# A decoder layer on one core: other column chunks in three stages, and another order of the three passes in two MLP groups

## The chip, the core and the metric

The kernel runs on one core of a Trainium2 chip. The core has a matrix engine (TensorE; PE in the profile, its weight loads PEld), a vector engine (DVE), a scalar engine (ACT), a general-purpose engine (POOL) and queues that issue transfers (SP's above all). The engines run side by side and wait for each other by semaphores. The metric is the device time of one execution in microseconds. Before the change three runs gave 2565.99, 2566.34 and 2569.97 us, a median of 2566.34.

## The reference

One layer of a decoder is applied to 1024 prompt tokens and to 64 sampled tokens (8 sequences of 8): 1088 columns in all, with 1024 channels. Four token mixers run in parallel on one input projection. The change touches only what follows them: the four branch projections with their gates, the output projection, and the MLP.

```python
branches = jnp.stack([y_hg, y_rw, y_cf, y_lru], axis=2).astype(dt)
bo = jnp.einsum("btkc,kcd->btkd", branches, p["w_branch"][l])
gates = jax.nn.sigmoid((h @ p["w_gate"][l] + p["b_gate"][l]).reshape(bsz, t, N_BRANCH, D_MODEL))
out = jnp.sum(gates * bo, axis=2) @ p["w_out"][l]
...
x = x + g1 * out
h2 = rmsnorm(x, p["norm_mlp_g"][l]) * (1.0 + sc2) + sh2
x = x + g2 * (jnp.square(jax.nn.relu(h2 @ p["w_mlp1"][l])) @ p["w_mlp2"][l])
```

Everything is float32, and the MLP's hidden layer has 4096 channels.

## The kernel before

Channels lie on the 128 partitions and tokens on the columns, so a tensor of 1024 channels is eight tiles (k-tiles) of 128 x 1088. A weight matrix is cut into 128 x 128 blocks. One output tile (an m-tile) is the sum over its k-tiles.

**Three passes.** Large products are computed from rounded operands. `split` (L206) writes `hi`, a rounded copy in the type float32r, with ACT, and `lo` = source - `hi` with DVE. `weights` (L148) fetches four k-tiles of weights at a time into `wst` and splits them into `whi` and `wlo`; there are three buffers for the first and four for each of the others. `products` (L158) then issues three matmuls for each k-tile into one sum: whi x hi, wlo x hi, whi x lo.

**Column chunks.** A PSUM bank holds 512 float32 columns, so 1088 columns are done in chunks. `CHUNKS` (L25) has 364, 362 and 362 columns. `gemm` (L169) goes over groups of four k-tiles, in each over the chunks, in each over four k-tiles of three passes, 12 matmuls for a chunk. The sums lie in the pool `pg`, which has three banks. After a chunk's last k-tile its evacuation reads the bank, with a high priority.

**Stages after the mixers.**

- Branch projections (L1131): four branches of eight m-tiles, four k-tiles each. DVE multiplies the sum by the gate `gt` and adds it to `M`.
- Output projection (L1168): eight m-tiles, eight k-tiles each. Before it, `M` is split into `Mh` and `Ml`, by `CHUNKS`: the first chunk of all eight k-tiles, then the second, then the third (L1160). The evacuation is `add_resid` (L1140), which adds the gated sum to the residual `R`, the 1024 prompt columns in one instruction and the 64 sampled columns in two, and `add_sq` (L1149), which squares `R` on ACT (into `sqt`) and adds it to `accs` on DVE.
- Second norm: `rms_finish` (L288) sums `accs` over the partitions on TensorE, by `CHUNKS`. ACT makes `rstd` of it, and DVE, POOL and ACT make `u`, then the MLP's input `Gh` and `Gl`.
- MLP: eight groups of 512 hidden channels. In each, four m-tiles of first products (L1223, eight k-tiles), whose evacuation is a ReLU and a square on ACT and two DVE instructions that leave `ah` and `al`; then eight m-tiles of second products (L1227, four k-tiles), evacuated by `add_resid`. Group 0 does its first two m-tiles chunk by chunk, and group 7's second products run by columns with the final norm behind them.

Code is written in program order; a scheduler of the framework sets each engine's order from priorities and its own estimates of time. Each engine then works strictly in that order.

Of the kernel before, what the change touches and what calls it, by code (L numbers as in the profile page):

```python
# [24 lines left out]
CHUNKS = ((0, 364), (364, 362), (726, 362))  # L25
DECAY = 0.606531
# [4 lines left out]
# packed per-channel parameters: name -> (first column, columns)  # L31
# [11 lines left out]
# constants that depend on shapes alone: name -> (first column, columns)  # L43
# [43 lines left out]
class Net:  # L87
    def __init__(self, ctx, tc, A):
        self.ctx, self.tc, self.nc, self.A = ctx, tc, tc.nc, A
        self.slots = list(range(13))  # L90

# [21 lines left out]
    def flat(self, name, slot):  # L113
        """one of this round's slots, each with a tile at a time"""
        return self.fp.tile([128, 1120], F32, name=name, tag=f"f{self.slots[slot]}", bufs=1)
# [32 lines left out]
    def weights(self, ap, prio=True):  # L148
        """four k-tiles of weights, rounded and remaining parts"""
        with self.tc.high_priority(offset=PRIO) if prio else nullcontext():  # L150
            st = self.wp.tile([128, 4, 128], F32, name="wst", tag="wst", bufs=WST)
            hi = self.wp.tile([128, 4, 128], F32R, name="whi", tag="whi", bufs=WHI)
            lo = self.wp.tile([128, 4, 128], F32R, name="wlo", tag="wlo", bufs=WHI)
            self.nc.sync.dma_start(st, ap)
            self.split(hi, lo, st)
        return hi, lo

    def products(self, ps, n0, n, W, X, k0, kt, nk=4):  # L158
        """nk k-tiles' three passes"""
        hi, lo = W  # L160
        xh, xl = X
        for k in range(k0, k0 + nk):
            i = k % 4
            a, b = xh(k)[:, n0:n0 + n], xl(k)[:, n0:n0 + n]
            self.mm(ps[:, :n], hi[:, i, :], a, start=k == 0, stop=False)
            self.mm(ps[:, :n], lo[:, i, :], a, start=False, stop=False)
            self.mm(ps[:, :n], hi[:, i, :], b, start=False, stop=k == kt - 1)
# [13 lines left out]
    def gemm_cols(self, items, X):  # L181
        """two m-tiles (weights, evacuation) of eight k-tiles, column chunk by column chunk"""
        Ws = [[self.weights(ap[:, k0:k0 + 4, :]) for k0 in (0, 4)] for ap, _ in items]
        for n0, n in CHUNKS:
            for W, (_, evac) in zip(Ws, items):
                ps = self.pgt("pg")
                for h in range(2):
                    self.products(ps, n0, n, W[h], X, 4 * h, 8)
                with self.tc.high_priority(offset=PRIO):
                    evac(ps, n0, n)  # L190

    def gemm_first(self, items, Ws, X):
        """two m-tiles of eight k-tiles, two k-tiles at a time, as they come"""
        pss = [[f("pg") for f in (self.pgt, self.pmt)] for _ in CHUNKS]
        for k in range(0, 8, 2):
            for (n0, n), pp in zip(CHUNKS, pss):
                for ps, W, (_, evac) in zip(pp, Ws, items):
                    self.products(ps, n0, n, W[k // 4], X, k, 8, 2)
                    if k == 6:
                        with self.tc.high_priority(offset=PRIO):  # L200
                            evac(ps, n0, n)
# [4 lines left out]
    def split(self, hi, lo, src):  # L206
        """src -> hi (rounded) and lo = src - hi, both float32r."""
        self.act(hi, src)
        self.tt(lo, src, hi.bitcast(F32), OP.subtract)

    def log_table(self, after=()):
        """from here on the activation table that has both Ln and Exp"""
        load = self.nc.scalar.preload_act_table_set("natural_log_exp_and_others")
        self.tc.keep_in_program_order(load)
        for i in after:
            self.after(load, i)
# [4 lines left out]
    def exph(self, out):  # L221
        """out holds ln(x); x^-1/2"""
        return self.act(out, out, AF.Exp, scale=-0.5)

    def after(self, i, j):
        """i is queued behind j"""
        self.tc.add_manual_dep(i.ins, j.ins.name, mybir.DependencyInfo(
            mybir.DependencyClass.NoSync, mybir.DependencyReason.DATA), reason="activation table")

# [8 lines left out]
    def ada_chunk(self, n, pool, pieces):  # L238
        """columns n*512..+512 of silu(c) @ ada_w + ada_b, channel-major into self.mod."""
        self.ada_sums(n, self.ada_parts(n, pool, pieces))  # L240
# [16 lines left out]
    def ada_sums(self, n, part, psum=None):  # L257
        """the first four chunks hold two k-tiles of shift, then the same two of scale"""
# [9 lines left out]
    def scale_from(self, g, sc, k0=0, n=8):  # L268
        """g * (1 + scale), in place in self.mod's columns sc*8+k0..+n"""
        m = self.mod[:, sc * 8 + k0:sc * 8 + k0 + n, :]  # L270
        g = PV[g] + k0
        self.stt(m, m, 1.0, self.pv[:, g:g + n].unsqueeze(2).to_broadcast([128, n, 9]), OP.add, OP.mult)
# [7 lines left out]
    def sumsq(self, acc, x, tmp):  # L280
        """acc += x^2 (acc = x^2 where tmp is None)"""
# [6 lines left out]
    def rms_finish(self, acc, out, chunks=CHUNKS):  # L288
        """out = rsqrt(sum over partitions of acc / D + eps), on every partition"""
# [6 lines left out]
    def split_mod(self, t, u, sc, sh, kb, hi, lo):  # L296
        """samples: u = t * scale + shift, split into hi + lo"""
# [6 lines left out]
    def rw_init(self):  # L304
# [9 lines left out]
        # scan resets: 0 where a chunk (or a sampled sequence) starts  # L314
# [6 lines left out]
        # (I - A)^-1 A of each head, the other head's rows 0  # L321
# [6 lines left out]
    def rw_shift(self, *jobs, Ws=None):  # L328
        """project m-tile mt, mix with the previous token: x + (prev - x) * mu"""
# [42 lines left out]
    def rw_block(self, j):  # L372
# [7 lines left out]
        # operands by chunk: (a~, r~) and (k~, b~), tokens innermost; eight chunks to a tile, then the samples  # L380
# [24 lines left out]
        # kk's norm  # L405
# [30 lines left out]
        # k' = k * (1 + (a - 1) ka)  # L436
# [6 lines left out]
        # scores within a chunk; rows k | b, columns a | r  # L443
# [25 lines left out]
        # bonus  # L469
# [6 lines left out]
        # (I - A)^-1 : 32 x 32 diagonal blocks, one per partition  # L476
# [19 lines left out]
        # X1: rows 64-95 the first block's inverse, rows 96-127 A12^T X1; the inverses (transposed) replace A in G  # L496
# [21 lines left out]
        # chunks  # L518
# [8 lines left out]
        for c in [16] + list(range(16)):  # L527
# [24 lines left out]
            # U = X (A_ak V + A S^T)  # L552
# [18 lines left out]
            # state  # L571
# [15 lines left out]
            # outputs  # L587
# [28 lines left out]
        # group norm over each head's values, bonus, gate  # L616
# [16 lines left out]
    def hg_init(self):  # L633
# [3 lines left out]
        # lower bound: cumsum(softmax over layers) - softmax[0]; one layer  # L637
# [10 lines left out]
    def hg_block(self, h):  # L648
# [20 lines left out]
        # scores, one level of halving at a time: X = [k exp(ref - b) | q exp(b - ref)]  # L669
# [67 lines left out]
        # decay to the chunk's start and end  # L737
# [146 lines left out]
    def lru_init(self):  # L884
# [8 lines left out]
        # softplus(-lambda) = max(-lambda, 0) + log1p(exp(-|lambda|)), with  # L893
        # log1p(e) = 2 atanh(z), z = e / (2 + e) <= 1/3, odd series to z^25
# [22 lines left out]
    def lru_block(self, j):  # L917
# [33 lines left out]
        # sqrt(-expm1(2 la)) with -expm1(2 la) = tanh(-la) (1 + exp(2 la)), la = -8 rg softplus(-lambda)  # L951
# [32 lines left out]
def trunk_kernel(ctx: ExitStack, tc: tile.TileContext, A):  # L984
# [14 lines left out]
    # ---- conditioning and the first norm  # L999
# [51 lines left out]
    # ---- input projection and the mixers  # L1051
    gsc = {}
    with ExitStack() as m:
# [32 lines left out]
        for j, order in enumerate(ROUNDS):  # L1086
            for st in order:
                steps[st](j)
            # a round's slots by its own numbers, in the order in which this one leaves them
# [8 lines left out]
    # ---- branch projections, gated and summed  # L1098
    mctx = ExitStack()
    merged = None  # L1100
    with ExitStack() as m:
# [5 lines left out]
        for bi, b in enumerate(ORDER):  # L1107
# [10 lines left out]
            for mt in range(8):  # L1118
# [11 lines left out]

                net.gemm(A["w_br"][b * 8 + mt], 4, Y, ev)  # L1131

    # ---- output projection, second norm
# [6 lines left out]
    def add_resid(ps, n0, n, mt, gi):  # L1140
        e = min(n, T - n0)
        r = R[mt]
        net.stt(r[:, n0:n0 + e], ps[:, :e], net.modp(gi, mt), r[:, n0:n0 + e], OP.mult, OP.add)
# [5 lines left out]
    def add_sq(n0, n, mt):  # L1149
        t = rp.tile([128, 364], F32, name="sqt", tag="sqt", bufs=2)[:, :n] if mt else None  # L1150
        net.sumsq(accs[:, n0:n0 + n], R[mt][:, n0:n0 + n], t)

    with ExitStack() as m:
# [9 lines left out]
        for mt in range(8):  # L1163
# [4 lines left out]
            net.gemm(A["w_out"][mt], KB8, (lambda k: Mh[k], lambda k: Ml[k]), ev)  # L1168
# [26 lines left out]
    # ---- MLP  # L1195
    with ExitStack() as m:
        ap_ = m.enter_context(tc.tile_pool(name="ap", bufs=1, reuse_waits="tile"))
        X2 = (lambda k: Gh[k], lambda k: Gl[k])
        for g in range(8):
# [21 lines left out]
            for i in range(i0, 4):  # L1221
                w, ev = first(i)
                net.gemm(w, KB8, X2, ev)  # L1223
            Y = (lambda k, ah=ah: ah[k], lambda k, al=al: al[k])
            if g < 7:
# [3 lines left out]
            # the last group by columns, so that the final norm runs behind the products  # L1229
# [110 lines left out]
```

## Time and profile before

| | |
|---|---|
| runs (median; all) | 2566.34; 2565.99, 2569.97, 2566.34 us |
| span of the profiled execution, first to last instruction | 2565.8 us |
| mean granted TensorE clock | 0.989 |
| branch projections | about 1451 to 1664 us |
| output projection, first to last matmul start | 1665.2 to 1763.0 us |
| MLP, from the first matmul start | 1766.9 us |

The page gives busy time of each engine, the chain of waits that ended last, and groups of instructions by line and tile. A name such as `pg<-Mh,whi` reads "writes a tile of pg, reads Mh and whi"; `128x364` is the shape that is written or read. All matmuls of the large products have line 103, that of a helper, so they are told apart by tiles. A matmul's length in the trace contains the time in which it overlaps the next one; the time from one start to the next is what a product costs.

### The profile page before, as it was taken

To read this page: it belongs to the slowest core of one execution; us is meant where nothing else is said; L and a number is where in the kernel's file an instruction comes from. 1 tells how busy PE (TensorE), PEld (TensorE's weight loads), DVE (VectorE), ACT (ScalarE), POOL (GpSimd) and SP (SyncE) were. 2 spreads that over 40 slices of the span, in tenths; PEclk is the share of its full clock that TensorE was granted. 3 is DMA by queue.
4 is the path that set the end of the run, shared out by engine and by line. 5 is a ranking of instruction groups with operands and counts; after the bars stand their busy time and mean duration, and the time that the engine had idled before them with its cause. 6 is when DMAs were issued, how large, how long until landed. Compare 5 with 4: busy or idle time off the path is not lost.

```text
span 2565.8 us, 43032 instructions
## 1 busy us (share of the span) xinstructions
PE 2488.8 (97%) x17874; PEld 2291.9 (89%) x17874; DVE 1339.9 (52%) x2506; ACT 916.2 (36%) x1644; POOL 248.8 (10%) x375
## 2 busy tenths in 40 slices
PE   6999999999999999999999999998999999999997
PEld 2897898897898978989887999998999999999997
DVE  6664626637265554457552756646534434434437
ACT  4522434323454224452244653334221221221225
POOL 3101110102100021000011000004000000000003
PEclk9999999999999999999999999999999999999998
DMA  6323131222222222212213454510111111111113
GB/s 238 121 78 78 53 104 65 64 85 72 90 69 66 70 86 93 65 61 79 85 53 109 167 193 158 185 42 26 50 46 46 42 46 46 46 42 46 46 42 110
DMA packets 112450, 209.23 MB, mean 82 GB/s; under 512 B 34408, under 2 KB 40504, under 8 KB 112256
## 3 DMA queue, kind: packets, MB, share of 16 engines
q1 hardware_dynamic: 98064, 166.93, 21.3%
q0 software_dynamic: 10880, 34.32, 3.5%
q10 hardware_dynamic: 3312, 5.25, 0.6%
q8 instruction: 140, 2.29, 0.4%
q14 instruction: 54, 0.44, 0.1%
HBM read 164.89 MB, written 41.55 MB: 80 GB/s over the span
## 4 chain that ended last, share of the span: by engine, by line
PE 83%; DVE 10%; DMA 3%; ACT 2%; issue 1%; POOL 0%; DVEq 0%; ACTq 0%; SPq 0%; POOLq 0%
PE pg L103 67%; PE sm L103 3%; DVE X L97 2%; PE ada L103 2%; PE pu L103 2%; DMA zx<-At 1%; PE pyr L103 1%; PE G L103 1%; DVE wlo L97 1%; PE tr L103 1%; PE po L103 1%; PE tr L537 1%; PE pst L103 1%; DVE Zu L97 1%; DVE tm L97 1%
## 5 line engine op out<-in xcount | busy, mean ns | idle before, releaser
L103 PE MATMUL pg<-Hh,whi 128*128 128x362 f32 (+1 forms) x1872 | 628.0, 336 | 4.6 <-ACT Hh L94 4.2
L103 PE MATMUL pg<-Hh,wlo 128*128 128x362 f32 (+1 forms) x1872 | 631.1, 337 | 0.0
L103 PE MATMUL pg<-Hl,whi 128*128 128x362 f32 (+1 forms) x1872 | 623.2, 336 | 0.7 <-DVE Hl L100 0.6
L94 ACT ACTIVATE whi<-wst 128x512 fp32r<-128x512 f32 x340 | 213.1, 628 | 730.9 <-PE pg L103 721.8
L97 DVE TENSOR_TENSOR wlo<-wst,whi 128x512 fp32r<-128x512 f32 x340 | 237.2, 699 | 428.7 <-ACT whi L94 427.3
L103 PEld LDWEIGHTS pg<-Hh,whi 128*128 128x128 f32 x1872 | 356.1, 190 | 15.2 <-ACT Hh L94 6.0
L103 PEld LDWEIGHTS pg<-Hh,wlo 128*128 128x128 f32 x1872 | 356.8, 191 | 13.8 <-issue 6.5
L103 PEld LDWEIGHTS pg<-Hl,whi 128*128 128x128 f32 x1872 | 355.2, 190 | 10.7 <-issue 2.5
L103 PE MATMUL pg<-Gh,whi 128*128 128x362 f32 (+1 forms) x768 | 253.4, 330 | 3.5 <-ACT Gh L94 2.6
L103 PE MATMUL pg<-Gl,whi 128*128 128x362 f32 (+1 forms) x768 | 252.4, 330 | 4.4 <-DVE Gl L97 4.0
L103 PE MATMUL pg<-Gh,wlo 128*128 128x362 f32 (+1 forms) x768 | 253.1, 330 | 0.1
L103 PE MATMUL pg<-ah,whi 128*128 128x362 f32 (+1 forms) x768 | 252.6, 329 | 0.5 <-DVE t L97 0.5
L103 PE MATMUL pg<-ah,wlo 128*128 128x362 f32 (+1 forms) x768 | 252.4, 329 | 0.0
L103 PE MATMUL pg<-al,whi 128*128 128x362 f32 (+1 forms) x768 | 250.1, 327 | 0.0
L100 DVE SCALAR_TENSOR_TENSOR R<-pg,mod,R 128x364 f32<-128x364 f32 (+2 forms) x216 | 123.6, 572 | 196.8 <-PE pg L103 196.8
L100 DVE SCALAR_TENSOR_TENSOR cacc<-u,pv,cacc 128x1024 f32<-128x1024 f32 x120 | 154.2, 1285 | 2.1
L103 PEld LDWEIGHTS pg<-Gl,whi 128*128 128x128 f32 x768 | 145.4, 190 | 7.6 <-DVE Gl L97 7.3
L103 PEld LDWEIGHTS pg<-Gh,whi 128*128 128x128 f32 x768 | 144.9, 189 | 4.9 <-ACT Gh L94 3.5
L103 PEld LDWEIGHTS pg<-Gh,wlo 128*128 128x128 f32 x768 | 144.9, 189 | 0.4 <-DVE wlo L97 0.4
L103 PEld LDWEIGHTS pg<-ah,whi 128*128 128x128 f32 x768 | 144.2, 188 | 1.1 <-ACT sqt L94 0.8
L103 PEld LDWEIGHTS pg<-al,whi 128*128 128x128 f32 x768 | 144.7, 189 | 0.1
L103 PEld LDWEIGHTS pg<-ah,wlo 128*128 128x128 f32 x768 | 144.3, 188 | 0.1
(383 smaller groups left out, 3698.7 us busy)
## 6 DMA issues: line engine op xcount, KB each, us to landing
wst<-w SPq DMA_DIRECT2D x136, 256.0 KB, 2.6
wst<-w_in SPq DMA_DIRECT2D x92, 256.0 KB, 2.9
gt<-g SPq DMA_DIRECT2D x32, 544.0 KB, 3.8
wst<-w_gate SPq DMA_DIRECT2D x64, 256.0 KB, 3.6
adaw<-ada SPq DMA_DIRECT2D x32, 512.0 KB, 4.4
g<-gst POOLq DMA_DIRECT2D x64, 181.0 KB, 2.2
yst<-y SPq DMA_DIRECT2D x16, 544.0 KB, 4.8
adaw<-ada SPq DMA_DIRECT2D x32, 256.0 KB, 5.4
```

The lines of the kernel that those rows point to most:

```text
L94: return self.nc.scalar.activation(out, in_, func, bias=bias, scale=scale)
L97: return self.nc.vector.tensor_tensor(out, a, b, op=op)
L100: return self.nc.vector.scalar_tensor_tensor(out, a, s, b, op0=op0, op1=op1)
L103: return self.nc.tensor.matmul(out, lhsT, rhs, start=start, stop=stop, skip_group_check=True)
L537: nc.tensor.transpose(ps[:, o + 128:o + 256], ch(kb, c + cc).rearrange("p a t -> p (a t)"), ident)
```

## The change

It does four things. The branch projections use chunks of 400, 400 and 288 columns. The output projection uses 512, 512 and 64, so that its third chunk holds the sampled tokens alone; `add_resid` then skips the empty prompt part, and `sqt` grows from 364 to 512 columns. The first products of MLP group 1 use four chunks of 272. From the second products of MLP group 3 to the first products of group 5 the passes stand in the order wlo x hi, whi x hi, whi x lo. Comments and docstrings are removed too, which shifts line numbers: what has line 103 before has line 107 after.

```diff
 CHUNKS = ((0, 364), (364, 362), (726, 362))
+CH_BR = ((0, 400), (400, 400), (800, 288))
+CH_OUT = ((0, 512), (512, 512), (1024, 64))
+CH_4 = ((0, 272), (272, 272), (544, 272), (816, 272))
...
+        self.hihi = False
...
             a, b = xh(k)[:, n0:n0 + n], xl(k)[:, n0:n0 + n]
-            self.mm(ps[:, :n], hi[:, i, :], a, start=k == 0, stop=False)
-            self.mm(ps[:, :n], lo[:, i, :], a, start=False, stop=False)
-            self.mm(ps[:, :n], hi[:, i, :], b, start=False, stop=k == kt - 1)
+            terms = ((lo, a), (hi, a), (hi, b)) if self.hihi else ((hi, a), (lo, a), (hi, b))
+            for j, (w, x) in enumerate(terms):
+                self.mm(ps[:, :n], w[:, i, :], x, start=k == 0 and j == 0, stop=k == kt - 1 and j == 2)
...
-                net.gemm(A["w_br"][b * 8 + mt], 4, Y, ev)
+                net.gemm(A["w_br"][b * 8 + mt], 4, Y, ev, CH_BR)
...
-        net.stt(r[:, n0:n0 + e], ps[:, :e], net.modp(gi, mt), r[:, n0:n0 + e], OP.mult, OP.add)
+        if e:
+            net.stt(r[:, n0:n0 + e], ps[:, :e], net.modp(gi, mt), r[:, n0:n0 + e], OP.mult, OP.add)
...
-        t = rp.tile([128, 364], F32, name="sqt", tag="sqt", bufs=2)[:, :n] if mt else None
+        t = rp.tile([128, 512], F32, name="sqt", tag="sqt", bufs=2)[:, :n] if mt else None
...
-            net.gemm(A["w_out"][mt], KB8, (lambda k: Mh[k], lambda k: Ml[k]), ev)
+            net.gemm(A["w_out"][mt], KB8, (lambda k: Mh[k], lambda k: Ml[k]), ev, CH_OUT)
...
-                net.gemm(w, KB8, X2, ev)
+                net.gemm(w, KB8, X2, ev, CH_4 if g == 1 else CHUNKS)
             Y = (lambda k, ah=ah: ah[k], lambda k, al=al: al[k])
+            net.hihi = g in (3, 4)
```

How the scheduler orders this is shown at three places. The first is TensorE where the branch projections end and the output projection begins. `yh` and `yl` are the last branch's input, `Mh_15940` and `Ml_15948` the two parts of the output projection's first k-tile, and the last number is the width in columns. Before:

```order
L103 MATMUL pg<-yh,whi 128x362
L103 MATMUL pg<-yh,wlo 128x362
L103 MATMUL pg<-yl,whi 128x362
L103 MATMUL pg<-Mh_15940,whi 128x364
L103 MATMUL pg<-Mh_15940,wlo 128x364
L103 MATMUL pg<-Ml_15948,whi 128x364
L103 MATMUL pg<-Mh_15941,whi 128x364
```

And in the changed kernel:

```order
L107 MATMUL pg<-yh,whi 128x288
L107 MATMUL pg<-yh,wlo 128x288
L107 MATMUL pg<-yl,whi 128x288
L107 MATMUL pg<-Mh_15940,whi 128x512
L107 MATMUL pg<-Mh_15940,wlo 128x512
L107 MATMUL pg<-Ml_15948,whi 128x512
L107 MATMUL pg<-Mh_15941,whi 128x512
```

The order is the same. What changes is that a 512-column product reads the first and the second piece of `Mh` and `Ml` (364 and 362 columns), and ACT and DVE still make the first pieces of all eight k-tiles before the first of the second pieces.

The second place is DVE where the output projection ends and the second norm begins. `R_15935` is the last m-tile of the residual, `accs` the sum of squares, `u` the scaled residual, and `Gl` the remainder part of the MLP's input. Before:

```order
L100 SCALAR_TENSOR_TENSOR R_15935<-pg,mod,R_15935 128x298
L97 TENSOR_TENSOR t_16816<-pg,mod 128x64
L97 TENSOR_TENSOR wlo<-wst,whi 128x512
L97 TENSOR_TENSOR R_15935<-R_15935,t_16816 128x64
L100 SCALAR_TENSOR_TENSOR u<-R_15928,mod,rstd_16846 128x364
L100 SCALAR_TENSOR_TENSOR u<-R_15930,mod,rstd_16846 128x364
L100 SCALAR_TENSOR_TENSOR u<-R_15932,mod,rstd_16846 128x364
L97 TENSOR_TENSOR accs<-accs,sqt 128x362
L100 SCALAR_TENSOR_TENSOR Gl_16835<-u,mod,Gh_16827 128x364
```

And in the changed kernel:

```order
L101 TENSOR_TENSOR t_16808<-pg,mod 128x64
L101 TENSOR_TENSOR R_15935<-R_15935,t_16808 128x64
L101 TENSOR_TENSOR accs<-accs,sqt 128x512
L101 TENSOR_TENSOR wlo<-wst,whi 128x512
L101 TENSOR_TENSOR accs<-accs,sqt 128x64
L104 SCALAR_TENSOR_TENSOR u<-R_15928,mod,rstd_16838 128x364
L104 SCALAR_TENSOR_TENSOR u<-R_15930,mod,rstd_16838 128x364
L104 SCALAR_TENSOR_TENSOR u<-R_15932,mod,rstd_16838 128x364
L104 SCALAR_TENSOR_TENSOR Gl_16827<-u,mod,Gh_16819 128x364
```

The last sum into `accs` has moved ahead of the three `u`, and has 64 columns; the 298-column update of the prompt is gone.

The third place is TensorE in the first products of group 5, where `Gh_16819` and `Gl_16827` are the two parts of the first k-tile of the MLP's input. In the changed kernel:

```order
L107 MATMUL pg<-Gh_16819,wlo 128x362
L107 MATMUL pg<-Gh_16819,whi 128x362
L107 MATMUL pg<-Gl_16827,whi 128x362
L107 MATMUL pg<-Gh_16820,wlo 128x362
L107 MATMUL pg<-Gh_16820,whi 128x362
L107 MATMUL pg<-Gl_16828,whi 128x362
```

Two products with `whi` of the same k-tile follow each other there; before, a product with `wlo` stood between them. In the first products of group 1 (not shown, since its rows only repeat) the three banks take the first three chunks of 272; the fourth chunk's 24 products stand behind the others' last ones and take the bank of the first.

## The prediction

> **What bounds the kernel now.** I read the page first, then busy time by stretch, then the stretches around the edited stages in order of time. The page's span, its busy row and its chain of waits:
>
> ```profile
> span 2565.8 us, 43032 instructions
> ...
> PE 2488.8 (97%) x17874; PEld 2291.9 (89%) x17874; DVE 1339.9 (52%) x2506; ACT 916.2 (36%) x1644; POOL 248.8 (10%) x375
> ...
> PE 83%; DVE 10%; DMA 3%; ACT 2%; issue 1%; POOL 0%; DVEq 0%; ACTq 0%; SPq 0%; POOLq 0%
> ```
>
> TensorE is the bound almost everywhere. So the question is what the same multiplications cost in other pieces. The busy time by stretch (after the bounds: length, then PE, weight loads, DVE, ACT, POOL, each with its count, then the granted clock) gives the branch projections, the output projection, the head of the MLP, and a quiet piece of the MLP:
>
> ```profile
> 1451.00:1664.00 213.00, 208.43 (x1396) 203.18 (x1382) 135.49 (x234) 85.97 (x100) 3.59 (x9) 1.00 0.54 184
> 1665.20:1763.20 98.00, 97.50 (x577) 97.20 (x578) 47.42 (x97) 30.14 (x61) 0.00 (x0) 0.98 0.15 44
> 1763.20:1803.00 39.80, 29.77 (x139) 24.37 (x138) 38.50 (x80) 23.53 (x50) 29.43 (x24) 0.91 0.03 7
> 2000.00:2500.00 500.00, 500.00 (x3013) 500.00 (x3012) 203.84 (x414) 112.96 (x216) 0.00 (x0) 1.00 0.15 45
> ```
>
> The last row gives the price of one product now: 500 us / 3013 = 166.0 ns for 362.67 columns on average, so 498.0 ns for the three chunks. DVE is 41% busy there. In the third row it is the other way round: DVE is busy 38.50 of 39.80 us and TensorE waits for it.
>
> How the 166.0 ns split is seen where the clock was halved, just after the output projection began (instructions in order of time: start, length, engine; the last row is busy time by stretch again):
>
> ```profile
> 1663.73 0.33 PE L103 MATMUL pg<-yl,whi 128*128 128x362 f32 x1
> 1665.22 0.43 PE L103 MATMUL pg<-Mh,whi 128*128 128x364 f32 x1 [1.17 <-ACT Mh L94]
> 1665.49 0.33 PE L103 MATMUL pg<-Mh,wlo 128*128 128x364 f32 x1
> 1666.30 0.67 PE L103 MATMUL pg<-Ml,whi 128*128 128x364 f32 x1 [0.48 <-DVE Ml L97]
> 1666.77 0.51 PE L103 MATMUL pg<-Mh,whi 128*128 128x364 f32 x1
> ...
> 1667.98 0.51 PE L103 MATMUL pg<-Mh,wlo 128*128 128x364 f32 x1
> ...
> 1666.30:1669.70 3.40, 3.40 (x11) 3.40 (x12) 3.40 (x8) 3.40 (x10) 0.00 (x0) 0.50 0.21 77
> ```
>
> From 1666.77 to 1667.98 lie four products of 364 columns: 302.5 ns each, 0.831 ns a column, at clock 0.50. At full clock a column would then take 0.4155 ns and 362.67 columns 150.7 ns. Measured are 166.0, so **15.3 ns of each product are not explained by its columns**. I take them as a fixed price of a product. My width law is then 0.4155 N + 15.3: 512 columns 228.0, 400 181.5, 288 135.0, 272 128.3 ns.
>
> The law must have a floor, since each product loads its own 128 x 128 weights. The nearest rows with few columns (duration lines by shape, then one run in order of time):
>
> ```profile
> L103 PEld LDWEIGHTS pg<-Ml,whi 128*128 128x128 f32 x192 | 36.6, 191 | 0.8 <-DVE Ml L97 0.8
> ...
> L103 PEld LDWEIGHTS po<-hq,sst 128*128 128x128 f32 x64 | 7.4, 191 | 0.3
> ...
> L103 PEld LDWEIGHTS pu<-St,wz 128*64 128x64 f32 x240 | 18.4, 136 | 4.1
> ...
> L103 PE MATMUL po<-hq,sst 128*128 128x8 f32 x64 | 7.8, 257 | 0.0
> ...
> 434.83 1.95 PE L103 MATMUL po<-hq,sst 128*128 128x8 f32 x16
> ```
>
> Sixteen products of 8 columns with full weights take 1.95 us; less the last one's 0.257 that is 1.69 / 15 = 113 ns from start to start, though 8 columns are nearly nothing. So 113 ns is what a load costs when nothing hides it. The loads of the large products last the same 191 ns, and 64 weight columns fewer make 55 ns less, so I carry 113 ns over as the floor. By the law 64 columns would take 41.9 ns; the floor holds, and I price them at **113 ns**.
>
> **The change, part by part.** The counts come from these rows (three passes of each kind):
>
> ```profile
> L103 PE MATMUL pg<-Mh,whi 128*128 128x362 f32 x128 | 41.9, 328 | 0.0
> ...
> L103 PE MATMUL pg<-Mh,whi 128*128 128x364 f32 x64 | 21.8, 341 | 1.2 <-ACT Mh L94 1.2
> ...
> L103 PE MATMUL pg<-yh,whi 128*128 128x362 f32 x256 | 85.2, 333 | 0.2 <-DVE gt L97 0.2
> ...
> L103 PE MATMUL pg<-yh,whi 128*128 128x364 f32 x128 | 42.7, 333 | 3.6 <-DVE gt L97 3.6
> ```
>
> *Output projection, 512/512/64:* 64 x 3 = 192 sets of three products. A set costs 2 x 228.0 + 113 = 569.0 instead of 498.0 ns, +71.0; times 192 is **+13.6 us**. Bounds for the 64-column product: 41.9 ns if nothing floors it (the set stays at 498, 0.0 us), and 166 ns if it costs what a product costs now (+23.8 us). I take 113, since that row has the same load and even fewer columns. Evacuation stays covered: DVE is 47.42 of 98.00 us busy, and a bank is wanted again only after the other two chunks, for the first one 12 x 228 + 12 x 113 ns = 4.1 us.
>
> *Branch projections, 400/400/288:* 128 x 3 = 384 sets; 2 x 181.5 + 135.0 = 498.0 ns, **0.0 us**. A law with no fixed price (166.0 / 362.67 per column) also gives 498.0. The same columns pass through DVE in as many instructions.
>
> *First products of MLP group 1, four of 272:* 4 m-tiles x 8 k x 3 passes = 96 sets, each 4 x 128.3 = 513.2 instead of 498.0: **+1.5 us**. There are three banks for four chunks, so the fourth chunk's 24 products stand last and reuse the first one's bank; in between lie 24 other products, 3.1 us, and what frees the bank is one ACT instruction:
>
> ```profile
> L94 ACT ACTIVATE rl<-pg 128x362 f32<-128x362 f32 x51 | 24.2, 474 | 49.8 <-PE pg L103 49.8
> ```
>
> 0.47 us against 3.1: hidden. If not, 4 x 0.5 us.
>
> *Pass order in groups 3 and 4* (second products of 3, all of 4, first products of 5): the same products, 384 triples, with the remainder weights first. They are split ahead; nothing new is waited for. **0.0 us.**
>
> *Entry to the output projection.* The first product now reads 512 columns, that is two of the pieces that ACT and DVE split by 364/362/362, first piece of all eight k-tiles before the second:
>
> ```profile
> 1664.68 7.62 ACT L94 ACTIVATE Mh<-M 128x364 fp32r<-128x364 f32 x19
> ...
> 1665.72 5.90 DVE L97 TENSOR_TENSOR Ml<-M,Mh 128x364 fp32r<-128x364 f32 x13
> ```
>
> ACT makes one in 0.401, DVE one in 0.454 us. The ninth is needed instead of the first: the first product can start 8 x 0.401 = 3.2 us later, and the third pass, which reads the remainder, 8 x 0.454 = 3.6 us later. The third pass sets what follows: **+3.6 us**. Behind it the next k-tiles come faster than TensorE uses them (0.454 against 3 x 0.228 us). The half clock in that stretch costs 3.40 - 11 x 0.166 = 1.6 us now; a longer idle time could double that or move it. I leave it at 0 and put +/-2 us into the range.
>
> *Exit to the MLP.* DVE bounds it, so its sum counts. Rows in order of time around TensorE's last product, 1763.1 us:
>
> ```profile
> 1762.58 0.54 DVE L97 TENSOR_TENSOR accs<-accs,sqt 128x362 f32<-128x362 f32 x1 [0.64 <-ACT sqt L94]
> ...
> 1763.35 0.53 DVE L100 SCALAR_TENSOR_TENSOR R<-pg,mod,R 128x298 f32<-128x298 f32 x1 [0.24 <-PE pg L103]
> ...
> 1764.62 0.22 DVE L97 TENSOR_TENSOR R<-R,t 128x64 f32<-128x64 f32 x1
> ...
> 1765.56 3.04 DVE L100 SCALAR_TENSOR_TENSOR u<-R,mod,rstd 128x364 f32<-128x364 f32 x3 [0.72 <-ACT rstd L94]
> ...
> 1768.53 1.28 DVE L97 TENSOR_TENSOR accs<-accs,sqt 128x362 f32<-128x362 f32 x1
> ```
>
> The 298-column update (0.53) and the late sum (1.28, behind the three `u`) go. In come a 512-column sum, 0.54 x 512/362 = 0.76, and a 64-column sum of about 0.22: 0.98 - 1.81 = **-0.8 us**.
>
> **Sum:** 13.6 + 0.0 + 1.5 + 0.0 + 3.6 - 0.8 = +17.9 us on the span of 2565.8, which is 2583.7. The median shown, 2566.34, lies 0.5 above the span; with that, **2584.2 us**.
>
> **Rivals.**
>
> *A product costs a constant until its columns need more.* Widths 362 and 364 alone can't tell a fixed price from a constant 166 ns (both last about 328 to 333 ns above). Then 512 columns take 212.7, 400 166.2, and 288, 272 and 64 take 166: output 192 x 93.4 = +17.9, group 1 96 x 166 = +15.9, branches 384 x 0.4 = +0.2, and +2.8 at the two ends: 2603. Against it: the 113 ns of the 8-column products, with the same load. Chance 0.12.
>
> *The 15.3 ns belong to these widths, and the kernel gets faster.* 364 and 362 are no multiples of 16; 512, 400, 288, 272 and 64 are. If the 15.3 ns vanish there, a set of the branches takes 2 x 166.2 + 119.7 = 452.1 ns, -45.9 x 384 = -17.6 us; group 1 (4 x 113 - 498) x 96 = -4.4; the output (2 x 212.7 + 113 - 498) x 192 = +7.8; the ends +2.8: -11.4, 2555. It decides as soon as the extra falls below about 6 ns (-11.4 us plus 1.92 us for each nanosecond). Against it: the 364-wide chunk starts at column 0 and is no cheaper than the others, and at half clock nothing is over even at 364. Chance 0.08. The Trainium skill, page "TensorE: Matmul & The Clock Gate", section "Back-to-back issue gap", has a rule of this kind: full-clock products in a row follow each other after N/2.4 + 2.5 ns. For 362 columns that is an estimate of 153 ns where this trace has 166, so the trace disagrees at the widths it has, and the new widths aren't in it. By that rule at the new widths alone the result would be an estimate of 2560 us.
>
> *Repeated weights cost less.* In the changed groups two passes with the same weights follow each other. If the second load fell away with its 15.3 ns, 384 x 15.3 = -5.9 us: 2578. Against it: the page counts as many loads as products, x17874 each. Chance 0.05.
>
> *No floor under 64 columns:* the output stage costs 0.0, in all 2570.6. Against it the 113 ns. Chance 0.05.
>
> **How the numbers follow.** Forecast 0.70, then 0.12, 0.08, 0.05, 0.05. The range leaves out the first two rivals (0.20): low is the case without a floor, 2570; high is 64 columns at 166 ns, 2584.2 + 10.2, and 2 us of half clock, 2596. A measurement of this kernel tells about 0.2% (5.1 us) from no change: faster 0.08, within it 0.05, slower 0.87.
>
> **What would show it.** Steps between starts of products: 228 ns at 512 columns, 113 at 64, 181.5/135 in the branches, 128 at 272, and 166 still in groups 3 to 5; the output stage at 98.0 + 13.6 us; the first product of it about 4.7 us after the last of the branches, where 1.5 lie now. Wrong would be: 64 columns clearly under or over 113, steps at 288 or 272 that stay at 166, fewer weight loads than products, or half clock for more than 7 us at the entry.

## The result and the profile after

The changed kernel took 2580.9, 2581.5 and 2589.64 us, a median of 2581.5 against 2566.34 before: +15.2 us. The ratio estimated from all runs is 1.0066 with a 95% interval of 1.0040 to 1.0092, that is +10 to +24 us. The profiled execution took 2581.5 us, with a span of 2579.5. The page's span, its busy row and its chain:

```profile
span 2579.5 us, 43218 instructions
...
PE 2502.3 (97%) x17970; PEld 2288.6 (89%) x17970; DVE 1340.3 (52%) x2506; ACT 916.5 (36%) x1652; POOL 248.7 (10%) x375
...
PE 86%; DVE 8%; DMA 3%; ACT 2%; issue 1%; POOL 0%; ACTq 0%; DVEq 0%; SPq 0%
```

TensorE has 96 products more (the fourth chunk of 272) and is 13.5 us longer busy; the other engines' busy time has hardly moved. Loads are still as many as products, 17970 each. The stages, from starts of TensorE's products in the two traces:

| stage | before | after | difference | forecast |
|---|---|---|---|---|
| up to the first branch product (code not changed) | 1451.70 | 1450.26 | -1.4 | 0 |
| branch projections | 212.03 | 211.46 | -0.6 | 0.0 |
| last branch product to first output product | 1.49 | 4.63 | +3.1 | 3.2 of the 3.6 |
| output projection, first to last product | 97.76 | 111.08 | +13.3 | 13.6 and the rest of the 3.6 |
| last output product to first MLP product | 3.87 | 3.50 | -0.4 | -0.8 |
| MLP, first to last product | 781.01 | 780.90 | -0.1 | +1.5 |
| tail | 17.88 | 17.66 | -0.2 | 0 |
| span | 2565.75 | 2579.50 | +13.8 | +17.9 |

Nearly all of it lies at the entry to the output projection and in it. In both profiles 3.41 us of half clock fell on the output projection. Busy time by stretch (columns as before: bounds, length, PE, loads, DVE, ACT, POOL, clock) gives the entry, the output projection, the first products of group 1 in four of 272, those of group 2 in 364/362/362, and the whole MLP:

```profile
1661.90:1666.30 4.40, 0.11 (x1) 0.00 (x0) 4.22 (x10) 4.20 (x11) 0.00 (x0) 1.00 0.18 60
1666.30:1777.60 111.30, 110.65 (x577) 94.55 (x577) 42.31 (x82) 25.41 (x53) 0.00 (x0) 0.98 0.11 36
1890.36:1938.50 48.14, 48.14 (x385) 48.14 (x385) 19.19 (x41) 16.82 (x38) 0.00 (x0) 1.00 0.14 40
1986.43:2034.20 47.77, 47.77 (x289) 47.77 (x289) 17.48 (x33) 15.18 (x30) 0.00 (x0) 1.00 0.16 45
1780.90:2561.80 780.90, 772.02 (x4707) 767.95 (x4708) 360.02 (x729) 209.17 (x408) 39.43 (x35) 1.00 0.16 46
```

In the first row TensorE waits while DVE and ACT are busy 4.2 of 4.4 us. In the second it is busy nearly all the time (110.65 of 111.30 us) but its loads are busy for only 94.55 us, where the row of before had 97.20 of 98.00: 512-column products leave a pause between loads. The third row has 384 products in the place of 288 and is only 0.4 us longer than the fourth (each count holds one product of the next block).

The entry and the last 64-column run in order of time (start, length, engine, shape, and in brackets how long it idled and for whom):

```profile
1661.72 0.29 PE L107 MATMUL pg<-yl,whi 128*128 128x288 f32 x1
1666.35 0.50 PE L107 MATMUL pg<-Mh,whi 128*128 128x512 f32 x1 [4.34 <-ACT Mh L98]
1666.68 0.40 PE L107 MATMUL pg<-Mh,wlo 128*128 128x512 f32 x1
1667.68 0.80 PE L107 MATMUL pg<-Ml,whi 128*128 128x512 f32 x1 [0.61 <-DVE Ml L101]
...
1775.83 0.39 PE L107 MATMUL pg<-Mh,wlo 128*128 128x512 f32 x1
1776.06 0.39 PE L107 MATMUL pg<-Ml,whi 128*128 128x512 f32 x1
1776.28 0.19 PE L107 MATMUL pg<-Mh,whi 128*128 128x64 f32 x1
1776.31 0.28 PE L107 MATMUL pg<-Mh,wlo 128*128 128x64 f32 x1
1776.42 0.28 PE L107 MATMUL pg<-Ml,whi 128*128 128x64 f32 x1
...
1777.43 0.28 PE L107 MATMUL pg<-Ml,whi 128*128 128x64 f32 x1
1777.54 0.86 PE L107 MATMUL rms<-accs,ones 128*128 128x364 f32 x2
```

From 1661.72 to 1666.35 are 4.63 us, and the third pass starts 5.96 us after the last branch product, where 2.57 lay before. Two 512-column products lie 0.23 us apart. From 1776.31 to 1777.43 are ten steps, 112 ns each, though 64 columns are an eighth of 512. The first step of such a run, 28 ns, comes out short, and the first 512-column step behind a run long (317 ns in this stage). The steps given below are therefore means from the second product of a run to its last, at full clock.

### The profile page after: what moved, and what is told of

Read it like the earlier page. It is cut to its first block, busy times and chain, and to the rows that moved or that the text cites. A ratio compares the mean times of both kernels' runs of the same rounds, so it can differ in the third digit from the quotient of the medians.

```text
span 2579.5 us, 43218 instructions
## 1 busy us (share of the span) xinstructions
PE 2502.3 (97%) x17970; PEld 2288.6 (89%) x17970; DVE 1340.3 (52%) x2506; ACT 916.5 (36%) x1652; POOL 248.7 (10%) x375
## 4 chain that ended last, share of the span: by engine, by line
PE 86%; DVE 8%; DMA 3%; ACT 2%; issue 1%; POOL 0%; ACTq 0%; DVEq 0%; SPq 0%
PE pg L107 70%; PE sm L107 3%; PE ada L107 2%; PE pu L107 2%; DVE X L101 2%; DMA zx<-At 1%; PE pyr L107 1%; PE G L107 1%; PE tr L107 1%; PE po L107 1%; DVE wlo L101 1%; PE tr L541 1%; PE pst L107 1%; DMA yst<-y 1%; PE p L107 0%
## 5 line engine op out<-in xcount | busy, mean ns | idle before, releaser
L107 PEld LDWEIGHTS pg<-Hh,wlo 128*128 128x128 f32 x1872 | 356.0, 190 | 13.8 <-issue 6.5
L107 PE MATMUL pg<-Gl,whi 128*128 128x362 f32 (+2 forms) x800 | 257.8, 324 | 8.3 <-DVE Gl L101 6.2
L107 PE MATMUL pg<-Gh,whi 128*128 128x362 f32 (+2 forms) x800 | 259.0, 324 | 0.4 <-ACT Gh L98 0.4
L107 PE MATMUL pg<-Gh,wlo 128*128 128x362 f32 (+2 forms) x800 | 258.8, 324 | 0.0
L104 DVE SCALAR_TENSOR_TENSOR R<-pg,mod,R 128x364 f32<-128x364 f32 (+3 forms) x208 | 122.0, 586 | 193.8 <-PE pg L107 193.7
L107 PEld LDWEIGHTS pg<-Gl,whi 128*128 128x128 f32 x800 | 151.3, 190 | 11.1 <-DVE Gl L101 8.6
L107 PEld LDWEIGHTS pg<-Gh,whi 128*128 128x128 f32 x800 | 151.3, 189 | 1.2 <-ACT Gh L98 1.0
L107 PEld LDWEIGHTS pg<-Gh,wlo 128*128 128x128 f32 x800 | 151.3, 189 | 0.2 <-DVE wlo L101 0.2
```

The source lines that it names most:

```text
L104: return self.nc.vector.scalar_tensor_tensor(out, a, s, b, op0=op0, op1=op1)
L107: return self.nc.tensor.matmul(out, lhsT, rhs, start=start, stop=stop, skip_group_check=True)
```

## The experiments

**The output projection alone, and everything but it.** The first kernel is the one before with the new chunks in the output projection only; the second is the changed one with the old chunks there.

```diff
-            net.gemm(A["w_out"][mt], KB8, (lambda k: Mh[k], lambda k: Ml[k]), ev)
+            net.gemm(A["w_out"][mt], KB8, (lambda k: Mh[k], lambda k: Ml[k]), ev, CH_OUT)
```

> The changed kernel with only the output projection's chunks (512/512/64) changed. Theory (512 columns cost 226.6 ns, 64 cost the 112 ns of a weight load, and the entry waits for two pieces instead of one): the output stage is 13 us longer (98 to 111 us from first to last product), the entry 3.1 us later, the exit to the MLP 0 to 1 us shorter, in all +15 to +16 us, 2581 to 2582. Rival (the loss of the changed kernel is spread over all edits): less than +10 us here.

> The changed kernel with the output projection back at 364/362/362; branches at 400/400/288, group 1 at four of 272 and the other pass order stay. Theory: branches 384 sets x (2 x 180.8 + 133.1 - 498.0) = -1.3 us, group 1 96 x (4 x 125.5 - 498.0) = +0.4 us, pass order 0; so 2565 to 2566, no change from before. Rival (the pass order or the 272s cost or save something of their own): 3 us or more away from before, with steps other than 166 ns in groups 3 to 5.

Alone it took 2585.68 us (4 runs) against 2568.61 of the kernel before on the same chip: +17.1 us by the medians, and by the ratio of 1.0059 (1.0044 to 1.0074) +15 us. Without it 2568.83 against 2568.61, 1.0004 (0.9991 to 1.0016). So the output projection with its entry carries the whole difference, and branches, group 1 and pass order together are worth nothing that 10 runs can tell (-2 to +4 us). Its stage is the same in both places: entry 4.66 us and 111.89 us from first to last product alone, 4.63 and 111.08 in the changed kernel, 1.45 and 96.07 without. Half clock fell on 6.83, 3.41 and 0 us of these three stages.

**The law of widths.** The kernel before with another set of chunks in each block of the MLP's groups 1 to 6:

```diff
+W1_PLAN = {1: plan(368, 368, 352), 2: plan(384, 352, 352), 3: plan(512, 512, 64), 4: plan(512, 384, 192),
+           5: plan(366, 362, 360), 6: plan(364, 364, 360)}
+W2_PLAN = {1: plan(512, 288, 288), 2: plan(368, 360, 360), 3: plan(512, 448, 128), 4: plan(512, 320, 256),
+           5: plan(272, 272, 272, 272), 6: plan(448, 320, 320)}
```

> The kernel before with another set of chunk widths in the first and second products of each of MLP groups 1 to 6: (368,368,352), (512,288,288); (384,352,352), (368,360,360); (512,512,64), (512,448,128); (512,384,192), (512,320,256); (366,362,360), four of 272; (364,364,360), (448,320,320). Theory (0.421 ns a column + 10.8 ns at widths that are multiples of 16, never under the 112 ns of a weight load): 128 and 192 columns step at 112, 256 at 118.6, 320 at 145.5, 352 at 159.0, 368 at 165.7, 384 at 172.5, 448 at 199.4; 360, 362, 364 and 366 about 2 ns above that line. Sets: (368,368,352) 490, (512,448,128) 538, (512,384,192) 511, (512,320,256) 491 ns against 498. Rival 1 (no floor, the same line all the way down): 192 at 92, 128 at 65. Rival 2 (the 2 ns at 362 are chance and no matter of the width): 352 at 161, 368 at 168.

Busy time of TensorE by stretch, one row for a block (length, busy time with count, clock): 368/368/352, 512/288/288, 368/360/360, 512/512/64, 512/448/128, 512/384/192, 512/320/256 and four of 272.

```profile
1878.19:1925.57 47.38, 47.38 (x289) 1.00 0.15 45
1925.65:1972.80 47.15, 47.15 (x290) 1.00 0.14 45
2020.47:2068.34 47.87, 47.87 (x290) 1.00 0.15 45
2068.42:2122.70 54.28, 54.28 (x289) 1.00 0.13 39
2122.81:2174.78 51.97, 51.97 (x290) 1.00 0.13 41
2174.89:2224.33 49.44, 49.44 (x289) 1.00 0.15 43
2224.44:2271.88 47.44, 47.44 (x290) 1.00 0.15 45
2319.68:2367.71 48.03, 48.03 (x385) 1.00 0.15 45
```

This kernel and the next two ran once each, so their stages and steps are read and not their times. All rows are 96 sets of 1088 columns (each count has an edge product or two). Against 498 ns for an ordinary set, the sets, from a block's first product to the next block's first, cost 494.4 ns (368/368/352), 492.5 (512/288/288), 499.5 (368/360/360), 567 (512/512/64), 543 (512/448/128), 516 (512/384/192), 495 (512/320/256) and 501.6 (four of 272). The theory had 490, 538, 511 and 491 ns for the four sets that it priced, 4 to 5 too low in each. Narrow runs of this kernel in order of time:

```profile
2094.35 0.28 PE L117 MATMUL pg<-Gh,wlo 128*128 128x64 f32 x1
...
2095.47 0.28 PE L117 MATMUL pg<-Gl,whi 128*128 128x64 f32 x1
...
2186.06 0.28 PE L117 MATMUL pg<-Gh,wlo 128*128 128x192 f32 x1
...
2187.17 0.27 PE L117 MATMUL pg<-Gl,whi 128*128 128x192 f32 x1
...
2235.04 0.28 PE L117 MATMUL pg<-ah,wlo 128*128 128x256 f32 x1
...
2236.24 0.28 PE L117 MATMUL pg<-al,whi 128*128 128x256 f32 x1
```

Ten steps take 1.12 us at 64 columns, 1.11 at 192 and 1.20 at 256. A product with 128 weight columns therefore costs 111 to 112 ns whether it has 64, 128 or 192 columns, and from 256 on its columns and a further price: 120.0 ns at 256, 125.4 at 272, 132.6 at 288, 146.5 at 320, 227.8 at 512. Less 0.4155 ns a column that leaves 13.6, 12.4, 12.9, 13.5 and 15.1 ns. "A constant 166 ns until the columns need more", "no floor" and "no fixed price at multiples of 16" all fall. What remains of the last is small: 362, 364 and 366 columns leave some 15 ns, and 272 and 288 some 2 to 3 ns less.

Between 352 and 368 columns the price does not rise in a straight line. Steps were 159.3 ns at 352 columns, 166.1 at 360, 165.7 at 362, 166.4 at 364, 166.7 at 366 and 167.5 at 368: the 8 columns from 352 to 360 cost 7 ns, the next 8 only 1 to 2. The first and third block above show it: 368/368/352 and 368/360/360 are both 1088 columns, and cost 494.4 and 499.5 ns. So 360 to 366 columns cost nearly as much as 368, as if widths were rounded up to a multiple of 16. No run has widths between 352 and 360, and the multiple of 16 is not the whole rule: 384 and 448 columns, at 176.0 and 203.0 ns, leave 16.4 and 16.8 ns, more than 288 or 320. The theory of the run (its line at multiples of 16, the widths between some 2 ns above) was right at 352 (159.0 expected) and wrong at 368 (165.7), where its rival's 168 came. The fixed price is thus no single number but 12 to 17 ns, and what sets it stays open.

That the floor is the load's is in part argued. For it speaks that it stays at 112 ns from 8 columns (the row of 16 products in the prediction, of which all steps but the first take 112) to 192, as long as the weights have 128 columns. Nor is 112 ns a least step of any product: in the trace of before, products with 64 weight columns follow each other much faster.

```profile
399.72 1.33 PE L103 MATMUL l<-X 128*64 128x64 f32 x36
```

These are 36 products in 1.33 us, four with 64 columns and 32 with 32 columns. They are small products of the mixers in plain float32; no run narrowed the weights of a narrow large product.

**Is the fixed price that of the weight load?** In the second products of groups 2, 3 and 4 the products behind the first of each sum use 64 weight columns (group 2), 32 weight columns (group 3) and 64 rows (group 4); the rest of these multiplications is left out.

```diff
+                r, c = self.part if k or j else (128, 128)
+                self.mm(ps[:c, :n], w[:r, i, :c], x[:r], start=k == 0 and j == 0, stop=k == kt - 1 and j == 2)
...
+                net.part = {2: (128, 64), 3: (128, 32), 4: (64, 128)}.get(g, (128, 128))
```

> The kernel before, but in the second products of MLP group 2 all products of a sum after its first use only 64 of the 128 weight columns, in group 3 only 32, and in group 4 only 64 of the 128 rows (so the outputs of these groups are partly left out). Widths stay 364/362/362. Theory (the 13 to 15 ns over the columns' own time belong to each product): steps stay at 166 ns in all three. Rival (they come from the weight load that runs beside the product): 64 weight columns step at about 158, 32 at about 155 ns, and 64 rows of full width stay at 166.

Steps, as means of a whole block, were 164.7 ns with 64 weight columns and 165.4 with 32, against 165.8 to 166.1 with 128. A load that is a half or a quarter takes away about 1 of 15 ns: the fixed price is not the load's. The 64 rows showed something that no expectation had named. In order of time, where the one full product of a sum stands between 64-row ones:

```profile
2223.52 0.32 PE L104 MATMUL pg<-ah,wlo 64*128 64x362 f32 x1
2223.69 0.32 PE L104 MATMUL pg<-al,whi 64*128 64x362 f32 x1
2223.93 0.43 PE L104 MATMUL pg<-ah,whi 128*128 128x362 f32 x1
2224.29 0.43 PE L104 MATMUL pg<-ah,wlo 64*128 64x362 f32 x1
2224.56 0.32 PE L104 MATMUL pg<-al,whi 64*128 64x362 f32 x1
2224.73 0.32 PE L104 MATMUL pg<-ah,whi 64*128 64x362 f32 x1
```

Steps of 0.17 us become 0.24, 0.36 and 0.27 around the full product: 0.87 us for three, 0.37 more than three ordinary ones. There are 24 such places in the block, which took 56.71 us up to the next block's first product instead of 47.84: 8.87 us, or 0.37 for each place. No such cost lies at the change between 64 and 128 weight columns.

**The entry, with pieces that fit.** The changed kernel with `M` split by the chunks that read it:

```diff
-        for n0, n in CHUNKS:
+        for n0, n in CH_OUT:
```

> The changed kernel, but M is split for the output projection in pieces of 512/512/64, as its products read it. Theory (the first product waits for the ninth piece on ACT, and the third pass for the ninth on DVE): the first product starts 1.5 to 1.7 us after the branches' last one instead of 4.6, the third pass 2.6 to 2.9 us instead of 6.0; the rest of the stage as in the changed kernel, 111 us. Rival (the entry waits for something else, the buffers or the last sum of the branches): still 4 us or more.

TensorE at the entry, in order of time:

```profile
1662.18 0.29 PE L107 MATMUL pg<-yl,whi 128*128 128x288 f32 x1
1663.75 0.50 PE L107 MATMUL pg<-Mh,whi 128*128 128x512 f32 x1 [1.29 <-ACT Mh L98]
1664.09 0.40 PE L107 MATMUL pg<-Mh,wlo 128*128 128x512 f32 x1
1664.71 0.50 PE L107 MATMUL pg<-Ml,whi 128*128 128x512 f32 x1 [0.23 <-DVE Ml L101]
```

First product after 1.58 us and third pass after 2.54, instead of 4.63 and 5.96, where 1.49 and 2.57 lay before: the whole of the added wait came from the mismatch between pieces and chunks. In this execution no half clock fell on the stage, and it took 109.35 us, less than the 111 expected. Of the 1.7 us by which the changed kernel's 111.08 is longer, 0.4 are a longer wait between its first product and its third pass; the other 1.4 lie behind that, where its half clock slows products that wait for nothing. Against the 96.07 us of the second experiment, also without half clock, the chunks cost 13.3 us.

**Can the fixed price be used?** By the steps 512/288/288 costs 492.5 instead of 498 ns a set. The kernel before with these chunks in gates, branches and MLP, and then in all stages:

```diff
+CH_W = ((0, 512), (512, 288), (800, 288))
...
-            net.gemm(A["w_gate"][b * 8 + mt], KB8, net.H, ev)
+            net.gemm(A["w_gate"][b * 8 + mt], KB8, net.H, ev, CH_W)
...
-                net.gemm(A["w_br"][b * 8 + mt], 4, Y, ev)
+                net.gemm(A["w_br"][b * 8 + mt], 4, Y, ev, CH_W)
...
-                net.gemm(w, KB8, X2, ev)
+                net.gemm(w, KB8, X2, ev, CH_W if 0 < g < 7 else CHUNKS)
...
-                    net.gemm(A["w2"][g, mt], 4, Y, lambda ps, n0, n: add_resid(ps, n0, n, mt, 5))
+                    net.gemm(A["w2"][g, mt], 4, Y, lambda ps, n0, n: add_resid(ps, n0, n, mt, 5), CH_W if g else CHUNKS)
```

> The kernel before with chunks of 512/288/288 in the gate products (32 m-tiles), the branch projections, and both products of MLP groups 1 to 6; everything else by 364/362/362. In the width run a set of 512/288/288 cost 492.5 ns where 364/362/362 costs 498.3. Theory (TensorE is the bound and the set price carries over): 768 + 384 + 576 + 576 = 2304 sets x -5.8 ns = -13 us, 0.5% faster than before. Rival (a longer chunk makes waits for its evacuation, or the entry to the output projection is late): -5 us or less.

> The kernel before with chunks of 512/288/288 everywhere, norms and mixers too. Theory (set price): 3984 sets x -5.8 ns = -23 us, less what the longer first pieces cost where VectorE bounds (entry to the output projection, head of the MLP, start of the program): -13 to -23 us. Rival (those pieces eat the gain): no better than the run with the chunks in selected stages.

Neither gain came, and the times are those of the two rivals: 2569.73 us, ratio 1.0001 (0.9992 to 1.0009), and 2570.62 us, 1.0004 (0.9996 to 1.0013). The reasons that the first rival gives don't fit its profile: the MLP was 7.0 us shorter (774.01 us) and the entry, 1.45 us, no later, but the first branch product came 5.7 us later (1457.39). This profile is of the fastest of the 12 runs (2562.54 us), so it doesn't show the whole of what the median lost. With all stages the step from the output projection to the MLP grew from 3.87 to 4.71 us and the tail from 17.88 to 19.22 besides. So the stages were taken one at a time: the MLP's edits alone, the gates' alone, the branches' alone, and MLP with branches. The next expectation names the second products of groups 1 to 7; the edit changes those of groups 1 to 6, and group 7's stay at 364/362/362.

> The kernel before with chunks of 512, 288 and 288 columns in the MLP's first products of groups 1 to 6 and second products of groups 1 to 7; gates, branches and output projection as before. In the run with these chunks in gates, branches and MLP the MLP was 7.0 us shorter than before (774.0 against 781.0 us), the time was not. Theory A: what ate the gain lies in the mixers' part, where the gate products fill gaps, so that without the gates' change the MLP's 7 us appear: about -6.5 us on the kernel before, ratio 0.9975. Theory B: nothing lies in the mixers, executions just differ by some us in the half-clock stretches (3.41 or 6.83 us each) and the shorter sets bring more of them: MLP shorter by 6 to 7 us in the profile, time within 2 us of the kernel before.

> The kernel before with chunks of 512, 288 and 288 columns in the gate products alone, which run between the mixers' own work. By the steps (227.5 + 2 x 132.4 ns for a set in place of 498) the gates' products would lose 5.6 ns a set on TensorE. Theory A: the time is longer than before, by 4 to 7 us, and the first product of the branches starts that much later. Theory B: within 2 us of the kernel before, the first product of the branches where it was (1450 to 1457 us in the profiles so far).

> The kernel before with chunks of 512, 288 and 288 columns in the MLP (as in the run with the MLP alone) and in the branch projections; gates and output projection as before. Theory A, each stage's gain stands by itself: 384 sets of the branches x 5.6 ns = 2.1 us more than the MLP alone, about -8.5 us on the kernel before, ratio 0.9967. Theory B, something other than the gates ate the gain in the run with gates, branches and MLP together: -4 us or less, ratio 0.9985 or more, and the MLP alone was better.

> The kernel before with chunks of 512, 288 and 288 columns in the branch projections alone. Theory A: -2.1 us, ratio 0.9992, hardly told from no change. Theory B, the branches are where gain was lost: longer by 2 us or more.

| 512/288/288 in | runs | median us | ratio, 95% interval | us by the ratio |
|---|---|---|---|---|
| MLP | 7 | 2561.00 | 0.9975, 0.9964 to 0.9987 | -6.4 |
| gates | 11 | 2573.31 | 1.0015, 1.0004 to 1.0026 | +3.9 |
| branches | 11 | 2570.45 | 1.0010, 1.0001 to 1.0019 | +2.6 |
| MLP, branches | 11 | 2564.50 | 0.9984, 0.9976 to 0.9993 | -4.1 |
| MLP, branches, gates | 12 | 2569.73 | 1.0001, 0.9992 to 1.0009 | +0.3 |

Theory A came for the MLP and, at its lower bound, for the gates; theory B came for the branches and, at its bound, for MLP with branches. The single effects add up to -6.4 + 3.9 + 2.6 = +0.1, near the +0.3 measured for the three together, though each is known to 2 or 3 us only. The MLP's gain is clear of the noise; the version with it alone, at 2561.0 us against 2567.67 on the same chip, is the fastest found. MLP with branches beats the kernel before too, by less. The gates lose although their products are shorter. TensorE and the others up to the first branch product, before:

```profile
0.00:1451.70 1451.70, 1407.51 (x11366) 1223.73 (x11367) 784.24 (x1430) 585.37 (x1071) 196.10 (x324) 0.99 0.27 87
```

and with the gates' chunks alone:

```profile
0.00:1458.40 1458.40, 1411.32 (x11366) 1195.62 (x11367) 783.29 (x1431) 586.19 (x1072) 201.00 (x324) 0.98 0.27 87
```

The same number of products; TensorE idles 47.1 instead of 44.2 us and is busy 3.8 us more at a lower clock. The idle time is outside the scatter: up to the first branch product it lies between 41.9 and 44.8 us in the ten profiles of kernels that leave the mixers' part as it was, and at 47.1, 49.3 and 45.7 us in the three with the gates' chunks changed (alone, with branches and MLP, and everywhere). It shows at the mixers' own small products: with the time to the next product counted in, those that write `lv` take 21.4 us instead of 16.8 to 17.6, and those for `pu` 50.1 instead of 46.9. The clock is the other part: over all runs its mean was 0.9855 with the gates' chunks and 0.9875 before (74 runs), and among runs of one kernel a thousandth less clock goes with 1.6 us more time, which would account for about 3.3 us; whether the gates' chunks bring the lower clock by the idle time, or otherwise, was not tried.

With the branches' chunks alone the clock explains 0.6 us (0.9871). In that profile the branches took 212.29 us, no less than the 212.03 before, with TensorE idle for 6.05 us of it; the six profiles with 364/362/362 there have 1.0 to 4.6 us. Most of the 6.05 are four waits of 0.5 to 1.7 us for DVE's evacuation into `M`. So waits ate the shorter steps in this execution. With the same chunks in three other kernels TensorE idled 3.5, 3.7 and 6.2 us in the branches, and why the kernel is slower than before stays open. Its first branch product came 3.8 us later, which is inside the scatter of that point.

## Why the prediction was right

- **Direction, size and place.** The median came out 2.7 us under the forecast, and on the span +13.8 were measured where +17.9 were forecast. The output projection alone gave +15 us, the rest nothing: the step that carried the forecast is the one that acted. That the total is so close is in part luck, since three runs of the changed kernel differ by 8.7 us; the terms below are the better test.
- **Output projection, +13.6:** 13.3 us without half clock. The floor of 113 ns, carried over from 8-column products with the same load, is 112 ns at 64 columns, and 512 columns cost 227.8 ns where 228.0 were forecast. The Trainium skill, page "TensorE: Matmul & The Clock Gate", section "LDWEIGHTS (loading the stationary operand)", gives P/1.2 for the load of P weight columns, an estimate of 107 ns for 128 of them. The steps of 112 ns lie 5 ns above that; the loads' own records, 191 ns, do not agree with it.
- **Entry, +3.6:** +3.4 at the third pass and +3.1 at the first product (4.63 us between the two products, 4.7 forecast), and gone when the pieces fit. The half clock was left out of the sum, and 3.41 us of it fell on the stage in both profiles. That was luck: the same chunks had 6.83 us of it in the first experiment and none with fitting pieces.
- **Branches, 0.0:** two of 400 and one of 288 cost 2 x 180.8 + 133.3 = 494.9 ns a set instead of 498, -1.2 us in 384 sets; 181.5 and 135.0 were forecast, both a little high. Not resolved in the time.
- **Group 1, +1.5:** +0.4 us. The law is 2 to 3 ns too high at 272 columns (125.5 measured, 128.3 forecast): its fixed price was taken from 362.67 columns, and the fixed price differs with the width.
- **Pass order, 0:** groups 3 to 5 still go at 165.8 to 166.1 ns, and loads equal products. In this kernel repeated weights save nothing.
- **Exit, -0.8:** -0.4 us up to the MLP's first product, but the forecast summed DVE's work, which the third pass behind it waits for. That pass starts 6.5 us after the last output product instead of 7.7, and the second products of group 0 begin 0.8 us earlier (65.1 instead of 65.9 us after it, with 6.83 us of half clock in both). Half of the forecast thus lies in the MLP's row of the table, where group 1 hides it.
- **What the sum missed.** The span's 4.1 us below the forecast are the untouched mixers (-1.4), the terms just named for branches, group 1 and exit together with the MLP's own start (-1.8), the entry and output stage (17.2 forecast, 16.5 measured, -0.7) and the tail (-0.2). Only the output stage with its entry stands out in repeated runs; the rest is inside the scatter: in the unchanged mixers' part alone the first branch product came between 1450.3 and 1457.1 us in ten profiles of kernels that don't touch it.
- **The rivals.** A constant 166 ns, no floor, and cheaper repeated weights are refuted above. The rival by which the 15.3 ns belong to these widths was right that multiples of 16 cost less, but 2 to 3 ns are gone at 272 and 288 columns where it would take 9. By the rule that the prediction cited of the Trainium skill, page "TensorE: Matmul & The Clock Gate", section "Back-to-back issue gap" (N/2.4 + 2.5), 512 columns would be an estimate of 215.8 ns and 256 one of 109.2; the trace has 227.8 and 120.0 and disagrees at every new width. The same section of the Trainium skill calls this the gap of single products, and says that in a stream of loads and products both set the spacing.

## What to carry to other kernels

Before cutting columns, price a chunk by numbers read from the trace: a step's floor, and its fixed part at widths near the new ones. A narrow leftover chunk pays the floor whatever its width (here 112 ns up to 192 columns), so three nearly equal chunks beat two full ones and a remnant (498 against 567 ns a set), and one wide with two equal ones was a little better still (492.5). When a consumer's chunks change, cut the producer's pieces alike, or the first product waits for pieces it doesn't otherwise need. A saving per product showed up in the time where TensorE hardly ever waited, in the MLP; in the gates, which share TensorE with the mixers' small products, and in the branches it did not, so it has to be measured in each stage.

## What was not expected of the hardware

- Full-height products between 64-row ones cost 0.37 us a place, though both shapes alone go at about 165 ns a step; products with 128 weight columns between those with 64 or 32 cost nothing extra.
- From 352 to 360 columns a step grows by 7 ns, from 360 to 368 by 1 to 2.
- The floor does not depend on the columns from 64 to 192 (112 ns at all three widths), and half the weight columns lower the step at 362 by only 1 ns.
- The mean granted clock of an execution of this one kernel varies between runs and between versions (0.9875 before, 0.9855 with other gate chunks, 0.9844 with 512/288/288 in all stages, in the mean of their runs). The half clock comes in stretches of 3.41 us or multiples of it, apart from the last one, which lasts to the end of the span. Among runs of one kernel a thousandth less mean clock goes with 1.6 us more time.
